# Copying PSUM banks into a transposed weight table with the tokens innermost, in a decoder layer's expert stage

## The chip, the cores and the metric

The kernel runs on one core of one Trainium2 chip. The metric is the device time of one execution in microseconds (us). TensorE (PE) multiplies and writes its products to PSUM, in banks of 512 fp32 columns; VectorE (DVE), ScalarE (ACT) and GpSimd (POOL) work beside it; SyncE (SP) and GpSimd issue the transfers. Each engine works through its own queue in order, and waits where an input or a buffer isn't ready.

## The reference

One decoder layer on 512 tokens of width 1024. A mixing part (sparse attention and a gated linear recurrence) gives `h`. Then comes the part that matters here, a retrieval over 16384 experts, each a row of `u` and a row of `v`:

```python
experts = jnp.take_along_axis(cand_idx..., pos, axis=-1)      # 8 heads x 16 per token
g = jax.nn.softmax(best, axis=-1)
h = jax.nn.gelu(jnp.einsum('td,thkd->thk', xb, u[experts]))
return jnp.einsum('thk,thkd->td', g * h, v[experts])
```

Every token picks 128 experts, and expert numbers are pairs (i, j) with i and j below 128. The result is added to the scaled `h` and normalised.

## The kernel before, in words

The 512 tokens are four blocks of 128. For blocks 0 and 1 the kernel gathers the chosen rows: `gather` lets GpSimd fetch one row of `u` or `v` per token (512 KB in all) into a tile `g`, VectorE multiplies and sums it (L665 for `u`, tile `gu`; L678 for `v`, tile `gv`). A generator, `peer_gather`, yields after each such row, and `pump(n)` in the other stages takes n of them. 52 of the v rows of block 0 go another way, through TensorE, in `pe_gather`: ScalarE makes a 128x128 diagonal `dg` with the gates of one choice (L694), and TensorE multiplies the gathered tile by it, two products of 512 columns (L696), summed in two banks (`pv` for the first 14 choices, `pw` for the other 38).

Blocks 2 and 3 (256 tokens) go through all 16384 experts densely, in `dense`. First the G stage builds a table G of shape [128 (i), 128 (j), 256 (token)], which holds the gate of expert (i, j) for every token. It takes four tokens at a time, a group; there are 64 groups. For each, VectorE compares `iota` with the token's 128 i and 128 j numbers and makes two tiles of one-hots `og` (L749); the second is multiplied by the gates, token by token, by ScalarE (L753), or for some tokens by VectorE (L755); TensorE multiplies the two for each of the four tokens into a bank `gb` laid out (token, j) (L758); ScalarE copies the bank of the group before into G (L736). Every second group one token of `pe_gather` follows, eight (PEPRE) having been taken before the stage; every third group (GPUMP) one row of block 1's `u` is pumped. `dtr` holds the transposed numbers and gates of the blocks, copied from PSUM by ScalarE (L727) just before.

Then the hidden stage runs over the 128 j: it streams 1 MB of `u` and `v` for each j, splits them into two parts, multiplies (L785), weighs with `G[:, j, :]` (L791) and multiplies again into four banks (L805). It pumps the remaining gathered rows on the way.

The gathered tiles share four buffers (tag `g`) in the G stage. `og` has 4 and 6 buffers, `gb` two, `dg` one; the `u` tiles of the hidden stage take over the buffers of `og`. The framework's planner orders the instructions of each engine and hands out buffers ahead of time, by a timeline of its own; where the text says `keep_in_program_order`, the order is as written.

Of the kernel before, what the change touches and what calls it, by code (L numbers as in the profile page):

```python
# [9 lines left out]
F32 = mybir.dt.float32  # L10
# [16 lines left out]
HGB = 5  # L27
GB = 4
UB = 4
VB = 3  # L30
HLB = 6
KB2 = 11
# [8 lines left out]
PEPRE = 8  # L41
PEG = 60

GACTS = (3, 4)

GPUMP = 3

# [4 lines left out]
def tile_decoder_layer(ctx, tc, a, out):  # L52
    nc = tc.nc

    cst = ctx.enter_context(tc.tile_pool(name="cst", bufs=1))
    gat = ctx.enter_context(tc.tile_pool(name="gat", bufs=5))
# [577 lines left out]
    def gather(table, b, k, nm):  # L634
        n = nth[0] % (GB + len(lent))
        nth[0] += 1
        if n < GB:
            t = gat.tile([128, 1024], F32, name=f"g{nm}{b}_{k}", tag="g", bufs=GB)
        else:
            t = cst.tile([128, 1024], F32, name=f"g{nm}{b}_{k}", tag=lent[n - GB])  # L640
        nc.gpsimd.indirect_dma_start(out=t, out_offset=None, in_=table,  # L641
                                     in_offset=bass.IndirectOffsetOnAxis(ap=idx[b][k // 64][:, k % 64:k % 64 + 1], axis=0))
        return t
# [42 lines left out]
    def pe_gather(n, p):  # L686

        while 0 not in weighted:
            pump(1)
        ks = [pe_left.pop(0) for _ in range(n)]  # L690
        for k in ks:
            g = gather(a["v"], 0, k, "v")
            dg = gat.tile([128, 128], F32, name=f"dg{k}", tag="dg", bufs=1)
            nc.scalar.mul(dg, ident, gate[:, 0, k:k + 1])  # L694
            for i in range(2):
                nc.tensor.matmul(p[i], dg, g[:, i * 512:(i + 1) * 512], start=(k == ks[0]), stop=(k == ks[-1]))  # L696
            if k != ks[-1]:
                yield
        for i in range(2):
            y = hs[0][:, i * 512:(i + 1) * 512]  # L700
            nc.vector.tensor_tensor(y, y, p[i], op=ALU.add)
        yield
# [4 lines left out]
    def pump(n):  # L707
        while n > 0 and todo:
            try:
                if not next(todo[0]):  # L710
                    return
                n -= 1
            except StopIteration:
                todo.pop(0)

    def dense(den, dps):
# [5 lines left out]
        for i, b in enumerate(DENSE):  # L722
            p = dps.tile([128, 512], F32, name=f"dtp{b}", tag="gb", bufs=2)
            for n, src in enumerate((keep[b][0], keep[b][1], gate[:, b, :])):
                nc.tensor.transpose(p[:, n * 128:(n + 1) * 128], src, ident)
            t = den.tile([128, 4, 128], F32, name=f"dtr{b}", tag="v", bufs=VB)
            nc.scalar.copy(t[:, 0:3, :].rearrange("p a b -> p (a b)"), p[:, :384])  # L727
            tr[b] = [t[:, n, :] for n in range(3)]
        pw = pe_gather(PEK2, [dps.tile([128, 512], F32, name=f"pw{n}", tag=f"acc0_{n}") for n in range(2)])
        for _ in range(PEPRE):  # L730
            next(pw)
        pdone = PEPRE
        G = den.tile([128, 128, T], F32, name="G")

        def evacuate(t0, p):
            nc.scalar.copy(G[:, :, t0:t0 + 4].rearrange("p j t -> p t j"), p)  # L736

        def pump_some(t0):
            if t0 // 4 % GPUMP == 0:
# [2 lines left out]
        for t0 in range(0, T, 4):  # L742
            p = dps.tile([128, 4, 128], F32, name=f"gb{t0}", tag="gb", bufs=2)
            x = tr[DENSE[t0 // 128]]
            c = t0 % 128
            og = [den.tile([128, 4, 128], F32, name=f"og{t0}_{n}", tag=tag, bufs=bufs)
                  for n, (tag, bufs) in enumerate((("u", UB), ("hl", HLB)))]
            for n in range(2):
                nc.vector.tensor_tensor(og[n], iota[:, None, :].to_broadcast([128, 4, 128]),  # L749
                                        x[n][:, c:c + 4, None].to_broadcast([128, 4, 128]), op=ALU.is_equal)  # L750
            gact = GACTS[t0 // 4 % len(GACTS)]
            for tt in range(gact):
                nc.scalar.mul(og[1][:, tt, :], og[1][:, tt, :], x[2][:, c + tt:c + tt + 1])  # L753
            if gact < 4:
                nc.vector.tensor_tensor(og[1][:, gact:, :], og[1][:, gact:, :],  # L755
                                        x[2][:, c + gact:c + 4, None].to_broadcast([128, 4 - gact, 128]), op=ALU.mult)
            for tt in range(4):
                nc.tensor.matmul(p[:, tt, :], og[0][:, tt, :], og[1][:, tt, :], start=True, stop=True)  # L758
            if t0:
                evacuate(t0 - 4, last)  # L760
            last = p
            pump_some(t0)
            while pdone < PEK2 and pdone < PEPRE + (t0 // 4 + 1) * (PEK2 - PEPRE) // PEG:
                next(pw)
                pdone += 1
        evacuate(T - 4, last)
        while 0 not in spent:
            pump(1)
# [10 lines left out]
        def into_hidden(j, n, hp):  # L779
            u = den.tile([128, 512], F32, name=f"u{j}_{n}", tag="u", bufs=UB)  # L780
            nc.sync.dma_start(u.rearrange("p (k i) -> p k i", k=4), a["ut"][j, :, n * 4:n * 4 + 4, :])
            uh, ul = split(f"u{j}_{n}", u)
            for q, (ut, ht) in enumerate(((uh, hTl), (uh, hTh), (ul, hTh))):
                for k in range(4):
                    nc.tensor.matmul(hp, ut[:, k * 128:(k + 1) * 128], ht[n][:, k, :],  # L785
                                     start=(n + q + k == 0), stop=(n == 1 and q == 2 and k == 3))
# [11 lines left out]
        def out_of_hidden(j, n, wh, wl):  # L798
            v = den.tile([128, 512], F32, name=f"v{j}_{n}", tag="v", bufs=VB)
            nc.sync.dma_start(v, a["v"][j * 128:(j + 1) * 128, n * 512:(n + 1) * 512])  # L800
            vh, vl = split(f"v{j}_{n}", v)
            for i in range(nb):
                sl = slice(i * 128, (i + 1) * 128)
                for q, (wt, vt) in enumerate(((wl, vh), (wh, vh), (wh, vl))):
                    nc.tensor.matmul(acc[i][n], wt[:, sl], vt, start=(j == 0 and q == 0), stop=(j == 127 and q == 2))  # L805

        def residual():
            ia = gat.tile([128, 128], F32, name="ia", tag="dg", bufs=1)
            nc.scalar.mul(ia, ident, ALPHA)
            for i in range(nb):  # L810
                for n in range(2):
                    for c in range(4):
                        for t in (hTl, hTh):
                            nc.tensor.matmul(acc[i][n][:, c * 128:(c + 1) * 128],
                                             t[n].bitcast(F32)[:, c, i * 128:(i + 1) * 128], ia,
                                             start=False, stop=False)
# [4 lines left out]
        for j in range(129):  # L821
            if j < 128:
                hp = dps.tile([128, 512], F32, name=f"hp{j}", tag="hp", bufs=2)[:, :T]
                into_hidden(j, 0, hp)
            want = total * min(j + 1, DLAST) // DLAST
            pump(want - due)
            due = want
            if j:
                out_of_hidden(j - 1, 0, *ws)
            if j == 2:  # L830
                residual()
            if j == DLAST:
                gb = ln2_consts(1)
                finish(1, gb)
            if j < 128:
                into_hidden(j, 1, hp)
                ws_new = weigh(j, hp)
            if j:
                out_of_hidden(j - 1, 1, *ws)
            ws = ws_new  # L840
# [5 lines left out]
    def stage(blocks, xT):  # L846
# [39 lines left out]
        if blocks != [0]:  # L886
            lent.clear()
            for part, tags in (("h", ("hx0", "hx1")), ("l", ("hs2", "hs3"))):
                hT_parts[part] = [cst.tile([128, 4, 256], F32R, name=f"hT{part}{i}", tag=tag) for i, tag in enumerate(tags)]
            for k in range(0, 8, 2):  # L890
                x = hT[:, k:k + 2, 128:384]
                th, tl = [hT_parts[part][k // 4][:, k % 4:k % 4 + 2, :] for part in "hl"]
                nc.scalar.copy(th, x)
                nc.vector.tensor_tensor(tl, x, th.bitcast(F32), op=ALU.subtract)
            for _ in pe_gather(PEK1, [bank(f"pv{i}", "hg") for i in range(2)]):
                pass
# [58 lines left out]
```

## Time and profile before

| what | value |
|---|---|
| time, median of 3 runs | 1610.61 us (1610.09 to 1612.2) |
| the profiled execution | 1619.35 us, span 1617.6 us |
| mean granted TensorE clock | 0.942 |
| busy share of the span: PE, DVE, ACT, POOL | 89%, 86%, 44%, 42% |
| DMA | 467.90 MB, 289 GB/s in the mean |

The span is the time from the first instruction to the last in one execution under the profiler; the time of that execution is a little longer than its span. The runs without a profiler are those of the median. PEld is TensorE's loading of weights, which overlaps its products. Shares over the whole span hide that the stages have different limits, so the rows further down are of single stretches.

### The profile page before, as it was taken

The page shows a single profiled execution, that of the slowest core. Times are in us where ns is not written, and L with a number is a line of the kernel's source. Part 1 is how long each engine was busy: PE and PEld are TensorE (multiplying, and loading weights), DVE is VectorE, ACT ScalarE, POOL GpSimd, SP SyncE. Part 2 cuts the span into 40 slices and gives each one's busy share as a digit, 9 for nine tenths or more (in the row PEclk, how much of TensorE's full clock was granted, in tenths as well). Part 3 has the DMA queues.
Part 4 walks back from the last instruction along what each step waited for, and adds up shares of the span by engine and source line. Part 5 has one row for each costly group of instructions (what it writes and reads, how often), then busy time and mean ns, then how long its engine had stood idle before and what let it go on. Part 6 is the DMA issues. An engine that isn't in the chain of part 4 may idle for free. (4 is left out here: it accounts for less than half of the span.)

```text
span 1617.6 us, 24516 instructions
## 1 busy us (share of the span) xinstructions
PE 1446.4 (89%) x7858; PEld 1090.0 (67%) x7858; DVE 1385.0 (86%) x3263; ACT 707.1 (44%) x1501; POOL 674.6 (42%) x531
## 2 busy tenths in 40 slices
PE   8997879755777799679989999999999999999996
PEld 4756534533443466236668888888888889989985
DVE  4219997888889889998887999899998999999998
ACT  3312121122332012249994555555555555555553
POOL 0000057757766440254443444444453346545440
PEclk9998989865789899999999999999999999999998
DMA  8454579989879871457678999999999999999995
GB/s 289 171 161 150 171 265 409 341 304 346 301 270 342 309 296 53 143 164 229 225 226 289 350 345 354 320 351 351 354 352 332 342 343 361 358 348 351 353 360 192
DMA packets 166162, 467.90 MB, mean 289 GB/s; under 512 B 18576, under 2 KB 18704, under 8 KB 165904
## 3 DMA queue, kind: packets, MB, share of 16 engines
q0 software_dynamic: 73728, 268.47, 47.4%
q1 hardware_dynamic: 92304, 197.86, 33.9%
q8 instruction: 62, 1.02, 0.2%
q14 instruction: 68, 0.56, 0.1%
HBM read 464.16 MB, written 2.10 MB: 288 GB/s over the span
## 5 line engine op out<-in xcount | busy, mean ns | idle before, releaser
L641 POOL DMA_INDIRECT gv<-in_v_dram,idx x256 | 340.8, 1331 | 400.4 <-DVE hs L678 237.5
L641 POOL DMA_INDIRECT gu<-in_u_dram,idx x256 | 323.0, 1262 | 433.3 <-DVE gu L665 193.0
L665 DVE SCALAR_TENSOR_TENSOR gu<-gu,hs 128x1024 f32<-128x1024 f32 x256 | 310.9, 1236 | 30.5 <-DMA gu<-in_u_dram,idx 30.0
L678 DVE SCALAR_TENSOR_TENSOR hs<-gv,gate,hs 128x1024 f32<-128x1024 f32 x204 | 261.5, 1282 | 12.1 <-DMA gv<-in_v_dram,idx 9.3
L774 ACT CAST v_0h<-v 128x512 fp32r<-128x512 f32 x128 | 79.7, 623 | 95.3 <-PE acc L805 57.9
L525 PE MATMUL pq<-hT,wpq 128*128 128x128 f32 (+1 forms) x512 | 118.4, 389 | 0.0
L774 ACT CAST v_1h<-v 128x512 fp32r<-128x512 f32 x128 | 79.5, 621 | 88.6 <-DMA v<-in_v_dram 40.2
L776 DVE TENSOR_TENSOR u_0l<-u,u_0h 128x512 fp32r<-128x512 f32 x128 | 88.5, 691 | 29.6 <-ACT u_0h L774 26.7
L774 ACT CAST u_0h<-u 128x512 fp32r<-128x512 f32 x128 | 79.3, 620 | 68.0 <-PE hp L785 32.1
L805 PE MATMUL acc<-v_0h,wl 128*128 128x512 f32 x256 | 102.0, 399 | 2.8 <-DVE wl L795 2.8
L776 DVE TENSOR_TENSOR v_1l<-v,v_1h 128x512 fp32r<-128x512 f32 x128 | 88.1, 688 | 17.2 <-ACT v_1h L774 13.9
L525 PEld LDWEIGHTS pq<-hT,wpq 128*128 128x128 f32 x512 | 79.9, 198 | 31.7 <-issue 1.1
L805 PE MATMUL acc<-v_0h,wh 128*128 128x512 f32 x256 | 101.2, 395 | 0.0
L774 ACT CAST u_1h<-u 128x512 fp32r<-128x512 f32 x128 | 79.4, 621 | 49.5 <-PE acc L805 42.1
L805 PE MATMUL acc<-v_1h,wl 128*128 128x512 f32 x256 | 100.3, 392 | 0.0
L805 PE MATMUL acc<-v_1h,wh 128*128 128x512 f32 x256 | 100.1, 391 | 0.0
L805 PE MATMUL acc<-v_0l,wh 128*128 128x512 f32 x256 | 99.7, 391 | 0.0
L776 DVE TENSOR_TENSOR u_1l<-u,u_1h 128x512 fp32r<-128x512 f32 x128 | 88.0, 687 | 5.8 <-ACT wh L793 2.3
L776 DVE TENSOR_TENSOR v_0l<-v,v_0h 128x512 fp32r<-128x512 f32 x128 | 88.2, 689 | 2.5 <-ACT v_0h L774 1.5
L785 PE MATMUL hp<-hTh,u_1l 128*128 128x256 f32 x512 | 84.8, 288 | 4.9 <-DVE u_1l L776 2.9
L785 PE MATMUL hp<-hTl,u_0h 128*128 128x256 f32 x512 | 83.8, 286 | 6.0 <-ACT u_0h L774 5.7
L785 PEld LDWEIGHTS hp<-hTl,u_0h 128*128 128x128 f32 x512 | 76.4, 189 | 18.6 <-ACT u_0h L774 8.8
(275 smaller groups left out, 3199.3 us busy)
## 6 DMA issues: line engine op xcount, KB each, us to landing
v<-in_v_dram SPq DMA_DIRECT2D x256, 256.0 KB
u<-in_ut_dram SPq DMA_DIRECT2D x256, 256.0 KB
wpq<-in_w_pq_dram SPq DMA_DIRECT2D x32, 512.0 KB
wo<-in_w_o_dram SPq DMA_DIRECT2D x16, 512.0 KB
hfw<-in_w_hf_dram SPq DMA_DIRECT2D x8, 512.0 KB
hqw<-in_w_hq_dram SPq DMA_DIRECT2D x8, 512.0 KB
hiw<-in_w_hi_dram SPq DMA_DIRECT2D x8, 512.0 KB
qaw<-in_w_qa_dram SPq DMA_DIRECT2D x8, 512.0 KB
```

The costliest lines, as they stand in the source:

```text
L525: nc.tensor.matmul(qp[:, :nt], w[:, k, :], hT[:, k, :nt], start=(k == 0), stop=(k == 7))
L641: nc.gpsimd.indirect_dma_start(out=t, out_offset=None, in_=table, in_offset=bass.IndirectOffsetOnAxis(ap=idx[b][k // 64][:, k % 64:k % 64 ...
L665: nc.vector.scalar_tensor_tensor(g, g, 1.0, hs[b], op0=ALU.mult, op1=ALU.mult, accum_out=hd[:, k:k + 1]))
L678: nc.vector.scalar_tensor_tensor(hs[b], g, gate[:, b, k:k + 1], hs[b], op0=ALU.mult, op1=ALU.add))
L774: nc.scalar.copy(h, x)
L776: nc.vector.tensor_tensor(l, x, h.bitcast(F32), op=ALU.subtract)
L785: nc.tensor.matmul(hp, ut[:, k * 128:(k + 1) * 128], ht[n][:, k, :], start=(n + q + k == 0), stop=(n == 1 and q == 2 and k == 3))
L805: nc.tensor.matmul(acc[i][n], wt[:, sl], vt, start=(j == 0 and q == 0), stop=(j == 127 and q == 2))
```

## The change

Three edits, all in the G stage or shared with it.

The copy of a bank into G goes through its elements in another order. Before, it went token by token, reading the bank in its own order and writing with a step of 256 elements (1024 bytes) between neighbours. Now it goes through j, and for each j through the four tokens: it writes four neighbouring elements of G, then steps by 256 elements, and reads the bank with a step of 128 elements (512 bytes). What ends up in G is the same.

ScalarE multiplies the one-hots of all four tokens of each group by the gates. Before, it took three in every even group and four in every odd one, and VectorE took the remaining one.

The diagonals `dg` get two buffers in place of one. The scaled identity of the residual (`ia`) shares them.

```diff
+DGB = 2
...
-GACTS = (3, 4)
+GACTS = (4,)
...
-            dg = gat.tile([128, 128], F32, name=f"dg{k}", tag="dg", bufs=1)
+            dg = gat.tile([128, 128], F32, name=f"dg{k}", tag="dg", bufs=DGB)
...
         def evacuate(t0, p):
-            nc.scalar.copy(G[:, :, t0:t0 + 4].rearrange("p j t -> p t j"), p)
+            nc.scalar.copy(G[:, :, t0:t0 + 4], p.rearrange("p t j -> p j t"))
...
-            ia = gat.tile([128, 128], F32, name="ia", tag="dg", bufs=1)
+            ia = gat.tile([128, 128], F32, name="ia", tag="dg", bufs=DGB)
```

## Rows read from the trace of the kernel before

**Rows 1.** Windows: length; busy us (instructions) of PE, PEld, DVE, ACT, POOL; clock; DMA.
```profile
640.00:713.00 73.00, 55.32 (x145) 23.92 (x143) 72.21 (x452) 20.01 (x39) 24.36 (x18) 0.95 0.41 123
713.00:850.00 137.00, 124.14 (x644) 84.77 (x644) 116.43 (x216) 131.34 (x324) 62.96 (x56) 0.99 0.71 228
870.00:1600.00 730.00, 720.11 (x4548) 648.37 (x4547) 673.88 (x1096) 389.94 (x757) 323.69 (x225) 1.00 0.96 343
```

**Rows 2.** Waits of PE, 870 to 1600: total us, times, longest.
```profile
PE hp L785 <- ACT u_0h L774: 4.0, 11, 0.9
```

**Rows 3.** Groups of ACT, 713 to 850: busy us, mean ns, idle before, releaser.
```profile
L753 ACT ACTIVATE og<-og,dtr 128x128 f32<-128x128 f32 x224 | 73.0, 412 | 0.0
L736 ACT COPY G<-gb 128x512 f32<-128x512 f32 x64 | 64.9, 1072 | 1.7 <-PE gb L758 1.7
L694 ACT ACTIVATE dg<-ident,gate 128x128 f32<-128x128 f32 x32 | 13.2, 412 | 5.5 <-PE pw L696 5.5
L727 ACT COPY dtr<-dtp 128x384 f32<-128x384 f32 x2 | 0.8, 469 | 0.0
```

**Rows 4.** Timeline of ACT, 795 to 800: start, us, what, times, idle before.
```profile
795.68 1.94 ACT L736 COPY G<-gb 128x512 f32<-128x512 f32 x2
797.41 1.27 ACT L753 ACTIVATE og<-og,dtr 128x128 f32<-128x128 f32 x4
798.58 0.40 ACT L694 ACTIVATE dg<-ident,gate 128x128 f32<-128x128 f32 x1
798.87 0.99 ACT L753 ACTIVATE og<-og,dtr 128x128 f32<-128x128 f32 x3
799.74 1.02 ACT L736 COPY G<-gb 128x512 f32<-128x512 f32 x1
```

**Rows 5.** Groups of ACT over the whole span, copies out of PSUM.
```profile
L455 ACT COPY PT<-pt 128x512 f32<-128x512 f32 x20 | 10.7, 591 | 6.0 <-PE pt L453 6.0
...
L527 ACT COPY pqs<-pq 128x128 f32<-128x128 f32 x16 | 4.3, 267 | 19.6 <-PE pq L525 19.6
```

**Rows 6.** Timeline of ACT at the start of the G stage.
```profile
712.93 0.84 ACT L727 COPY dtr<-dtp 128x384 f32<-128x384 f32 x2
715.16 0.40 ACT L694 ACTIVATE dg<-ident,gate 128x128 f32<-128x128 f32 x1 [1.39 <-PE pw L696]
...
722.26 1.06 ACT L736 COPY G<-gb 128x512 f32<-128x512 f32 x1 [1.08 <-PE gb L758]
```

**Rows 7.** Groups of DVE, 713 to 850.
```profile
L665 DVE SCALAR_TENSOR_TENSOR gu<-gu,hs 128x1024 f32<-128x1024 f32 x22 | 26.9, 1223 | 16.6 <-DMA gu<-in_u_dram,idx 16.6
L755 DVE TENSOR_TENSOR og<-og,dtr 128x128 f32<-128x128 f32 x32 | 9.1, 285 | 0.2
```

**Rows 8.** Timeline of PE before the stage, one token of 14 such.
```profile
672.97 1.98 PE L696 MATMUL pv<-gv,dg 128*128 128x512 f32 x4 [0.55 <-ACT dg L694]
```

**Rows 9.** Timeline of PE, 733 to 742.
```profile
734.14 1.88 PE L696 MATMUL pw<-gv,dg 128*128 128x512 f32 x4
735.86 1.95 PE L758 MATMUL gb<-og,og 128*128 128x128 f32 x16
737.64 1.88 PE L696 MATMUL pw<-gv,dg 128*128 128x512 f32 x4
```

**Rows 10.** Waits of DVE, 713 to 850: total us, times, longest.
```profile
DVE gu L665 <- DMA gu<-in_u_dram,idx: 16.6, 15, 3.1
```

**Rows 11.** Timeline of DVE, 800 to 832, the products with gathered u.
```profile
807.00 1.23 DVE L665 SCALAR_TENSOR_TENSOR gu<-gu,hs 128x1024 f32<-128x1024 f32 x1 [0.86 <-DMA gu<-in_u_dram,idx]
...
813.19 1.22 DVE L665 SCALAR_TENSOR_TENSOR gu<-gu,hs 128x1024 f32<-128x1024 f32 x1 [0.78 <-DMA gu<-in_u_dram,idx]
...
819.04 1.23 DVE L665 SCALAR_TENSOR_TENSOR gu<-gu,hs 128x1024 f32<-128x1024 f32 x1 [0.77 <-DMA gu<-in_u_dram,idx]
```

**Rows 12.** Timeline of POOL, two issues of gathers of u.
```profile
776.50 1.85 POOL L641 DMA_INDIRECT gu<-in_u_dram,idx  x1 [2.37 <-PE pw L696]
...
808.51 1.35 POOL L641 DMA_INDIRECT gu<-in_u_dram,idx  x1 [2.16 <-DVE og L755]
```

## Prediction

> **What bounds the kernel now.** I read the sums by stretch first [rows 1]. The edits touch the G stage, 713 to 850 us, where ScalarE is busy 131.3 of 137.0 us, TensorE 124.1 and VectorE 116.4. So ScalarE sets the pace there, with TensorE close behind. The stretch before it (640 to 713) belongs to VectorE, 72.2 of 73.0 us. The one behind it (870 to 1600) belongs to TensorE, 720.1 of 730.0 us, and its longest wait there on any one line is 4.0 us in all [rows 2]. That stretch runs a fixed amount of work and starts when G is full, so what the G stage gains or loses is passed on to the end about one for one.
>
> Next, the groups of ScalarE inside the stage [rows 3]: 224 weights of one-hots, 64 copies into G, 32 diagonals. Their idle times are 0, 1.7 and 5.5 us. Mean durations overlap their neighbours, so I take start to start from the timeline [rows 4]. Two copies start at 795.68 and the next weight at 797.41, so a copy takes 0.865 us of the engine. Four weights fill 797.41 to 798.58, 0.293 each; the diagonal takes 0.29; the pattern repeats at 799.74. A pair of groups (eight tokens) therefore costs 4.06 us. The sum, 64 x 0.865 + 224 x 0.293 + 32 x 0.29 = 55.4 + 65.6 + 9.3 = 130.3, with 0.8 for the two dtr copies, is the 131.3 of [rows 1].
>
> **The copies.** How much of 0.865 is due to the order of the elements? The same instruction with both sides contiguous stands elsewhere in the kernel [rows 5]: 512 columns out of PSUM take 591 ns, 128 columns 267, so 0.844 ns per column and a fixed 159. The copy into G moves the same 512 columns in 1072 ns [rows 3], 1.78 ns per column: about twice as much. Its read is contiguous; its write steps 1024 bytes from element to element, so the scattered write is what doubles it. After the edit the write has runs of four elements (16 bytes), and the read steps 512 bytes through a PSUM bank on every element. No row here shows ScalarE reading PSUM with such a step.
>
> So I bound it. Below: the contiguous price. Two dtr copies of mean 469 ns end 0.84 us after the first started [rows 3, 6], so the second started 0.37 us after the first and contiguous copies overlap by 0.10; the edited copy would take 0.591 - 0.10 = 0.49 us, and 64 of them give back 64 x 0.375 = 24.0 us. Above: the stepped read costs what the stepped write cost, 0.865, and nothing is given back. Both penalties at once (0.48 us more on top of 0.865, 31 us in all) is the far end; I leave it out of the forecast, since the write would have to keep its price although three of four elements follow their neighbour. I take 0.49: the only measured penalty goes with the write.
>
> [...]
>
> **The weights.** Every second group hands one weight from VectorE to ScalarE: 32 more at 0.293, so +9.4 us on ScalarE, and VectorE loses 32 x 285 ns = 9.1 us [rows 7]. VectorE isn't the bound by its busy time, so that gives nothing back by itself. ScalarE's new sum is 31.4 + 75.0 + 9.3 = 115.7, against 130.3: 14.6 us less, 3.61 us per pair.
>
> **The diagonals.** With one buffer, TensorE waits 0.55 us for each diagonal when it does nothing but such tokens: the product at 672.97 shows it, as do 13 more between 640 and 713 us [rows 8]. A second buffer removes this. Before 713 us that is worth nothing, because VectorE's routing covers it; without that cover it would be 14 x 0.55 = 7.7 us. At the stage's start it should help: ScalarE sits 1.39 us for a diagonal's buffer and 1.08 us for the first bank, because TensorE is still at the last two tokens of the eight taken in advance [rows 6]. I count 1 us of these 2.5: how much of them is TensorE's lateness and how much VectorE's first one-hots, the rows don't part. In the stage proper, ScalarE can place a diagonal earlier in its queue; as long as ScalarE is the bound that gives nothing. The residual's scaled identity shares this buffer and isn't waited for.
>
> **What is late next.** TensorE: a token (1.72) and eight products (1.78) run back to back from 734.14 to 737.64, 3.50 us for a pair [rows 9]. 30 pairs with a token and two without make 30 x 3.50 + 2 x 1.78 = 108.6 us. That is below 115.7, so it caps little. VectorE: 116.4 - 9.1 = 107.3 us busy, but it also waits 16.6 us for gathered rows of u, in 15 of 22 cases [rows 7, 10]. This is the cap that matters. In the second half of the stage each gather of u is issued right behind the product that used the one before: VectorE starts one at 807.00 and ends 1.15 us later; GpSimd issues the next at 808.51; it has landed at 813.19 [rows 11, 12]. The loop is 0.35 + 4.68 + 1.15 = 6.2 us, and 5.85 the next time (813.19 to 819.04), 6.02 on average, and the work of three groups that lies between two of them has 1.5 x 4.06 = 6.09 us now. Behind the waiting product stand VectorE's next one-hots, and behind these ScalarE's weights and TensorE's products. So where the gathers of u go round in one buffer, a faster ScalarE finds VectorE at 6.02 us per three groups, hardly faster than today. In the first half a gather of u also takes over the buffer of a v row, as the one at 776.50 does when a token's products are over [rows 12], and this loop doesn't bind.
>
> **The sum.** First half, 16 pairs: 16 x 0.45 = 7.2 us gained. Second half, 11 gathers: 11 x (6.09 - 6.02) = 0.8. Start: 1. Friction where ScalarE and TensorE come within 0.1 us of each other: I take 1 off. Together 8 us: the profiled span 1617.6 would become 1609.6. The profiled execution took 1619.35, 0.5% above the median of 1610.6; the G stage is a fixed piece of work, so I take the same 8 us off the median: 1602.5.
>
> **The rivals.**
> 1. *No gather loop binds.* The order of the gathers and who inherits which buffer are settled ahead by the framework's planner, and the edits change its input. If u gathers alternate buffers throughout, all 32 pairs gain 0.45, with the start 15 us: 1595 to 1599. For it: the first half before behaves so. Against it: the second half.
> 2. *The read takes the write's place* (the other side). The PSUM read with its 512-byte step costs two steps per element, the copy stays at 0.865, and 9.4 us of weights come on top: 1610.6 + 9.4 - 1 = 1619. It decides from a copy of 0.865 - 9.4 / 64 = 0.72 us start to start; above that the edit loses. [...] Against it: no row shows a slow PSUM read.
> 3. *The gather loop binds everywhere.* 22 x 6.02 = 132 us against the stage's 137: with the start and the tail the time moves by 0 to 3 us, 1607.5 to 1611. For it: VectorE already waits in 15 of 22 cases.
>
> **How the numbers follow.** The likeliest, 1598 to 1606 round 1602.5, has 0.36; rival 1 has 0.24; rival 3 has 0.17; rival 2 has 0.20; 0.03 is for a far worse copy. 0.2%, about what can be told from no change, is 3.2 us. Faster: 0.36 + 0.24 + a third of rival 3 = 0.66. Same: the rest of rival 3 and a copy near 0.72, 0.14. Slower: 0.20. The range: 1595 leaves out the lower end of rival 1 (0.05), and 1617 most of rival 2 and the far case (0.15). The likeliest's own range is 1598 to 1606.
>
> **What would show it.** The copy into G: about 590 ns mean, and 0.49 start to start, if the step on the PSUM side is free; 1070 if not. 256 weights on ScalarE, none on VectorE. ScalarE's busy sum in the stage near 116, its stage some 127 to 130 us long. VectorE's wait for rows of u grows from 16.6 us if the loop binds; if not, TensorE's idle in the stage shrinks instead. The 0.55 us before each diagonal's product is gone before 713, and the VectorE bound there unmoved. The prediction is wrong if the copy stays above 0.72, or if the stretch behind 870 us changes its own length.

## The result, and the profile after

The changed kernel takes 1638.69 us (median of 4 runs, 1632.59 to 1642.45) beside 1610.35 us for the kernel before on the same chip (4 runs): a ratio of 1.0171, 95% interval 1.0146 to 1.0196. It is 28 us slower where 8 us of gain was predicted, and lies above the range. The profiled execution took 1638.91 us, span 1637.2 us. All lines below the diagonals' buffer count stand one lower in the file than before: the copy into G is L737, the products L697 and L759, the one-hots L750.

I count the stage from the first copy into G to the last: 722.3 to 848.0 before, 125.7 us. In the changed kernel, by windows (columns as in [rows 1]):

```profile
640.00:713.00 73.00, 56.24 (x131) 24.20 (x129) 65.69 (x402) 19.25 (x42) 28.30 (x25) 0.91 0.56 178
713.00:863.00 150.00, 119.81 (x637) 86.48 (x638) 109.75 (x189) 117.52 (x348) 52.40 (x49) 0.94 0.58 181
720.40:861.90 141.50, 113.43 (x617) 82.31 (x617) 101.86 (x173) 115.48 (x343) 50.68 (x47) 0.96 0.60 187
884.00:1610.00 726.00, 714.26 (x4512) 643.53 (x4511) 666.07 (x1078) 385.23 (x750) 322.79 (x225) 1.00 0.96 344
```

The third row is the stage: 141.5 us, 15.8 more. No engine is busy for more than 115.5 of them. Before, ScalarE had 131.3 of 137.0 [rows 1]; now nobody has the stage. The last row is as before, TensorE busy 98% of it. Of the span's 19.6 us the stage holds 15.8; the first to the last weighing by G in the hidden stage takes 747.1 us beside 743.5, and 0.2 net lie at the start, the gap and the tail. The other 8.7 of the 28 us stand in no trace: the profiled execution of the kernel before took 1619.35 us, 9 above its median.

The groups of ScalarE, 713 to 863 us, against [rows 3]:

```profile
L754 ACT ACTIVATE og<-og,dtr 128x128 f32<-128x128 f32 x256 | 81.6, 395 | 4.0 <-DVE og L750 4.0
L737 ACT COPY G<-gb 128x512 f32<-128x512 f32 x64 | 36.0, 575 | 5.4 <-PE gb L759 4.8
L695 ACT ACTIVATE dg<-ident,gate 128x128 f32<-128x128 f32 x25 | 10.0, 398 | 22.9 <-PE pw L697 22.8
```

The copy fell from 1072 to 575 ns, and all 256 weights are ScalarE's. Its timeline, against [rows 4]:

```profile
739.78 0.56 ACT L737 COPY G<-gb 128x512 f32<-128x512 f32 x1
740.25 2.44 ACT L754 ACTIVATE og<-og,dtr 128x128 f32<-128x128 f32 x8
```

A copy is 0.47 us start to start (739.78 to 740.25), where 0.49 was forecast. So the copies do what they should; ScalarE waits instead, 22.9 us for the buffers of diagonals, which TensorE still reads. Who is late? The waits of all engines, 713 to 863 us (us in total, times, longest), against [rows 10]:

```profile
DVE og L750 <- PE gb L759: 40.1, 19, 4.8
POOL gu L642 <- DVE gu L666: 31.9, 7, 9.6
POOL gu L642 <- PE pw L697: 27.3, 9, 7.5
PE pw L697 <- DMA gv<-in_v_dram,idx: 26.6, 14, 4.4
ACT dg L695 <- PE pw L697: 22.8, 10, 4.8
```

VectorE's 16.6 us for rows of u are gone. It waits 40.1 us for TensorE to release the one-hots, TensorE waits 26.6 us for gathered rows of v, and GpSimd, which issues these, waits for VectorE and TensorE. That is a ring. One turn of it, first on TensorE:

```profile
820.16 1.99 PE L697 MATMUL pw<-gv,dg 128*128 128x512 f32 x4 [2.84 <-DMA gv<-in_v_dram,idx]
821.98 2.89 PE L759 MATMUL gb<-og,og 128*128 128x128 f32 x24
824.70 1.88 PE L697 MATMUL pw<-gv,dg 128*128 128x512 f32 x4
826.42 1.05 PE L759 MATMUL gb<-og,og 128*128 128x128 f32 x8
827.31 1.88 PE L697 MATMUL pw<-gv,dg 128*128 128x512 f32 x4
829.03 1.95 PE L759 MATMUL gb<-og,og 128*128 128x128 f32 x16
833.84 1.55 PE L697 MATMUL pw<-gv,dg 128*128 128x512 f32 x3 [2.87 <-DMA gv<-in_v_dram,idx]
```

then on VectorE:

```profile
823.07 2.50 DVE L750 TENSOR_TENSOR og<-iota,dtr 128x512 f32<-128x512 f32 x4 [2.96 <-PE gb L759]
825.48 1.22 DVE L666 SCALAR_TENSOR_TENSOR gu<-gu,hs 128x1024 f32<-128x1024 f32 x1
```

and on GpSimd:

```profile
826.98 1.15 POOL L642 DMA_INDIRECT gu<-in_u_dram,idx  x1 [3.63 <-DVE gu L666]
828.43 0.94 POOL L642 DMA_INDIRECT gv<-in_v_dram,idx  x1 [0.30 <-issue]
```

Follow the bracketed waits. TensorE's token at 820.16 and the first group behind it let VectorE write one-hots at 823.07 (2.91 us). Four of them stand in VectorE's queue ahead of the product with u at 825.48 (2.41). GpSimd wants that product's buffer for its next row of u and issues at 826.98 (1.50). The row of v that TensorE needs next has its own buffer, but stands behind in the same queue: 828.43 (1.45). It lands for TensorE at 833.84 (5.41). The sum is 13.68 us for six groups, 4.56 us a pair, where before a pair took 4.06. Also new are the 24, 8 and 16 products between tokens (3, 1 and 2 groups); before, it was 16 from the third gap on [rows 9]. TensorE's wait of 2.8 to 2.9 us ends at 806.50, at 820.16 and at 833.84, so this turn stands there twice in a row; earlier in the stage the order varies.

### The profile page after: what moved, and what is told of

It reads as the page before. It is cut to its first block, busy times and chain, and to the rows that moved or that the text cites. A ratio compares the mean times of both kernels' runs of the same rounds, so it can differ in the third digit from the quotient of the medians.

```text
span 1637.2 us, 24560 instructions
## 1 busy us (share of the span) xinstructions
PE 1455.2 (89%) x7858; PEld 1099.5 (67%) x7858; DVE 1378.4 (84%) x3231; ACT 695.0 (42%) x1533; POOL 671.0 (41%) x531
## 5 line engine op out<-in xcount | busy, mean ns | idle before, releaser
L642 POOL DMA_INDIRECT gu<-in_u_dram,idx x256 | 327.2, 1278 | 450.5 <-DVE gu L666 221.2
L642 POOL DMA_INDIRECT gv<-in_v_dram,idx x256 | 333.0, 1301 | 403.4 <-DVE hs L679 239.0
L750 DVE TENSOR_TENSOR og<-iota,dtr 128x512 f32<-128x512 f32 x128 | 81.1, 686 | 46.3 <-PE gb L759 40.1
L697 PE MATMUL pw<-gv,dg 128*128 128x512 f32 x152 | 82.3, 675 | 40.1 <-DMA gv<-in_v_dram,idx 33.1
L777 DVE TENSOR_TENSOR v_1l<-v,v_1h 128x512 fp32r<-128x512 f32 x128 | 88.0, 687 | 20.7 <-ACT v_1h L775 19.2
```

The source lines that it names most:

```text
L777: nc.vector.tensor_tensor(l, x, h.bitcast(F32), op=ALU.subtract)
```

## The experiments

**Theory**: the copy and the weights cost what was predicted; the stage is long because rings over the shared gather buffers close, and because the edits moved the order in which TensorE takes its tokens. **Rivals**: one of the edits is dear on its own engine (ScalarE's 115.7 us binds, or the weights cost more there), or TensorE's lower granted clock (0.94 in the second window beside 0.99 in [rows 1]) is the cause and not the result. All kernels compute the whole reference. "Stage" is the first to the last copy into G in the profiled execution; ratios are to the kernel before on the same chip, with 95% intervals. Medians of the kernel before move between 1610 and 1618 us from one batch of runs to the next, and single runs of one kernel by 10 to 23 us, so stages part the theories better than times, though each stage is that of one execution. The change itself was timed in the first batch alone. The first copy lies between 714.6 and 730.4 us (722.3 before), which the stage leaves out.

**One edit at a time.**

```diff
+DGB = 1
+GACTS = (3, 4)
```

(e1, the copy's order alone; e2 is the kernel before with `DGB = 2` alone; e3 is the copy with `GACTS = (4,)` and `DGB = 1`; e4 the copy with `GACTS = (3, 4)` and `DGB = 2`.)

> The copy's element order alone; weights and diagonals as before, and no instruction changes its place in any queue. If the ring of gathers behind the second diagonal buffer is the cause (theory A): ScalarE's 64 copies cost 575 ns in place of 1072 and the time falls by 5 to 13 us, 1598 to 1606. If any faster ScalarE runs into the gathers (theory B): the time stays or rises, 1608 to 1635, with TensorE waiting for rows of v as it does after the change.

> The second diagonal buffer alone; copy and weights as before. Theory A: slower by 15 to 30 us, 1626 to 1640, with TensorE's tokens waiting for rows of v some 20 to 30 us in the G stage. Theory B: within 5 us of before, since ScalarE still sets the pace at 4.06 us per pair.

> Copy and weights as in the change, one diagonal buffer. Theory A: faster than before by 5 to 14 us, 1596 to 1606. Theory B: near the changed kernel, 1625 to 1640. Theory C (the weights moved to ScalarE are what hurts): slower than the copy alone by 10 us or more.

> Copy and second diagonal buffer as in the change, weights shared with VectorE as before. Theory A: near the changed kernel, 1625 to 1642. Theory C: near the copy alone, 1598 to 1606.

| kernel | stage, us | ratio |
|---|---|---|
| before | 125.7 | 1 |
| e1, copy | 119.6 | 0.9976 (0.9944 to 1.0008) |
| e2, second diagonal buffer | 136.8 | 1.0074 (1.0039 to 1.0109) |
| e3, copy and weights | 133.6 | 1.0048 (1.0016 to 1.0080) |
| e4, copy and second buffer | 135.7 | 1.0089 (1.0063 to 1.0115) |
| the change | 141.5 | 1.0171 (1.0146 to 1.0196) |

The copy alone gains 4 us where theory A had 5 to 13, not clear of noise. e2 and e4 lose as theory A has it, but less: e2 11.7 us where 15 to 30 were expected, e4 about half of the change's loss. e3 goes against theory A, which had a gain, and meets theory C: it is 12.7 us slower than the copy alone, so the weights hurt too.

The second buffer, costed at nothing, makes the kernel before slower by itself. e2 and e4 have the same stage within 1.1 us although ScalarE is busy 125.9 us in the one and 105.6 in the other, so ScalarE doesn't set it. The waits of e2, 713 to 863 us, are of the kinds of the changed kernel; the most goes to rows of u that take over the buffer of a row of v and wait for TensorE's token (27.3 us in the changed kernel):

```profile
POOL gu L642 <- PE pw L697: 40.1, 12, 7.5
POOL gv L642 <- PE pw L697: 30.0, 16, 2.7
DVE og L750 <- PE gb L759: 25.1, 13, 5.2
PE pw L697 <- DMA gv<-in_v_dram,idx: 23.3, 13, 4.8
```

What the second buffer does to TensorE's queue can be counted in the timelines. In e2 and e4, 12 tokens stand ahead of the first group and the last 11 groups have no token between them; in the change it is 12 and 13, in the kernel before, e1 and e3 8 and 5. Between these ends e2 and e4 keep a token after every second group, as before, so the 3, 1 and 2 groups are not needed for the loss. The end of e2's tokens:

```profile
841.45 1.88 PE L697 MATMUL pw<-gv,dg 128*128 128x512 f32 x4
843.17 1.95 PE L759 MATMUL gb<-og,og 128*128 128x128 f32 x16
845.59 1.16 PE L759 MATMUL gb<-og,og 128*128 128x128 f32 x8 [0.47 <-ACT G L737]
```

e3 has another ring. Its waits and its window, 718.3 to 851.9 us:

```profile
POOL gu L642 <- DVE gu L666: 55.7, 15, 8.3
DVE gu L666 <- DMA gu<-in_u_dram,idx: 30.5, 18, 3.3
ACT og L754 <- DVE og L750: 18.6, 17, 2.4
```
```profile
718.30:851.90 133.60, 115.66 (x623) 81.09 (x621) 102.98 (x170) 113.57 (x342) 50.60 (x49) 1.00 0.65 210
```

Rows of u go round in one buffer from the stage's start to its end, 133.6 / 22 = 6.07 us a row. From one product with u to the next, over half of the turns take 5.9 to 6.3 us; four take 8.1 to 8.3, because a row of v has taken over u's buffer and the next row of u stands behind it (shown for e12 below). The shorter loop is the one that the prediction read at 6.02 [rows 11, 12] and let bind in the second half.

The clock here is 1.00 in a stage nearly as long as e2's. In the changed kernel it is lower only in pieces:

```profile
715.00:719.00 4.00, 3.88 (x6) 1.85 (x7) 4.00 (x8) 0.10 (x1) 0.00 (x0) 0.50 0.00 0
800.00:860.00 60.00, 46.55 (x280) 35.16 (x279) 48.01 (x84) 50.18 (x149) 22.17 (x20) 1.00 0.58 184
```

The turn shown above lies in the second piece, at 1.00: that ring isn't made by the clock. An estimate from the mean of 0.96 over the stage: the clock can hold at most 0.04 x 141.5 = 5.7 of its us.

**Buffers parted by use.** In the G stage, rows of v get two of the four buffers, rows of u two.

```diff
-            t = gat.tile([128, 1024], F32, name=f"g{nm}{b}_{k}", tag="g", bufs=GB)
+            tag = ("g", "gx")[nm == "u" if in_g[0] else n % 2]
+            t = gat.tile([128, 1024], F32, name=f"g{nm}{b}_{k}", tag=tag, bufs=GB // 2)
```

> The whole change, with the four gather buffers parted in the G stage: two for rows of v, two for rows of u (elsewhere they alternate). Theory A (the loss is the ring: rows of u and v inherit each other's buffers, so GpSimd's queue waits for VectorE and TensorE in turn): the G stage, first copy into G to last, falls from 141 us to 118 to 125 and the time is 10 us or more under the changed kernel's. Theory D (a stage this fast can't be fed with gathered rows, whoever inherits the buffers): the stage stays at 133 us or more, and TensorE's tokens still wait over 15 us for rows of v.

> The kernel before, with the buffers parted in the same way; the control for the run above. Both theories: ScalarE sets the pace at 4.06 us per pair, the stage stays at 124 to 130 us, and the time stays within 4 us of before.

> The copy's element order alone, with the buffers parted. Theory A: the stage falls below the 119.6 us of the copy alone, to 113 to 118, and the time is 3 to 6 us under the copy alone. Theory D: no better than the copy alone, 119 us or more.

On the change (e5) the stage falls only to 133.1 us, ratio 1.0060 (1.0032 to 1.0088). TensorE still waits for v, 20.7 us from 713 to 855, and GpSimd 49.7 us for TensorE to release a buffer: two are too few for v in that order. This is what theory D had. On the kernel before (e6): 129.6 us, 0.9976 (0.9954 to 0.9999). On the copy alone (e7): 122.0 us, 0.9959 (0.9933 to 0.9985); theory A had 113 to 118 for it.

**No rows of u in the stage.** `GPUMP = 64` moves 21 of the 22 rows of u from the G stage into the hidden stage.

> The whole change with all but one of block 1's 22 rows of u moved out of the G stage into the hidden stage, which gets them as extra work. Theory A: with rows of v alone in the four buffers nobody inherits from the other kind, and the G stage falls from 141 us to 113 to 122; the hidden stage grows. Theory D: TensorE still waits for rows of v and the stage stays above 130.

One run: 1624.7 us beside 1615.16. The stage is 124.8 us, above the 113 to 122 expected, and TensorE waits for no row of v in it. That fits rows of u closing the ring, but doesn't show it: the order of TensorE's tokens came out otherwise too (16 ahead of the first group, two after every second group, none between the last 43). The hidden stage takes 752.5 us between its first and last weighing, 5 to 16 more than in the others, with the 21 rows as extra work.

**A fifth gather buffer**, in the room of the hidden stage's split weights, which isn't in use yet: three for v, two for u.

```diff
+        if in_g[0] is not None:
+            in_g[1] += nm == "u"
+            if nm == "u" and in_g[1] % 2:
+                t = in_g[0].tile([128, 1024], F32, name=f"g{nm}{b}_{k}", tag="whl")
+            else:
+                t = gat.tile([128, 1024], F32, name=f"g{nm}{b}_{k}", tag="gx" if nm == "u" else "g", bufs=1 if nm == "u" else 3)
...
-            wh = den.tile([128, T], F32R, name=f"wh{j}", tag="wh", bufs=2)
+            wh, wl = (whl[0][:, 2 * k + j % 2, :].bitcast(F32R) for k in range(2))
```

(e9 is the change with it, e10 the copy alone, e11 the kernel before, e13 copy and weights, e14 copy and second diagonal buffer.)

> The whole change with a fifth gather buffer in the G stage (the room of wh and wl, which only the hidden stage uses): three buffers for rows of v, two for rows of u. Theory A (a ring of too few, shared buffers): no gather waits long for a buffer, TensorE's tokens wait under 6 us for rows of v in the stage, and the stage falls from 141 us to 116 to 124; the time is 15 us or more under the changed kernel's. Theory D (the gathers themselves are too slow for such a stage): over 130 us.

> The copy's element order alone, with the five parted buffers. Theory A: the stage, 119.6 us with the copy alone and 122.0 with four parted buffers, falls to 111 to 117, TensorE's sum being 108.6; the time is 8 to 16 us under before. Theory D: 119 or more.

> The kernel before with the five parted buffers, the control. Both theories: ScalarE's sum of 130 us keeps the stage at 124 to 128 us; the time stays within 5 us of before.

> Copy and weights as in the change, one diagonal buffer, five parted gather buffers. If the 133.6 us of copy and weights together are the loop of rows of u, the stage falls to ScalarE's own sum, 115 to 119 us; the 32 weights then cost 5 to 9 us against the copy alone with the same buffers (109.8). If the weights hurt by something else, 125 or more.

> Copy and second diagonal buffer as in the change, weights shared, five parted buffers. If the planner's order of the tokens costs by itself (tokens taken early, bare groups left for the end), the stage is 115 to 122 us against 109.8 without the second buffer; if the second buffer hurts only through the ring of gathers, 108 to 112.

| kernel | stage with 4, us | stage with 5, us | ratio with 5 |
|---|---|---|---|
| before (e11) | 125.7 | 125.2 | 1.0011 (0.9990 to 1.0033) |
| copy (e10) | 119.6 | 109.8 | 0.9918 (0.9892 to 0.9943) |
| copy and weights (e13) | 133.6 | 118.5 | 0.9985 (0.9962 to 1.0008) |
| copy and second buffer (e14) | 135.7 | 127.7 | 1.0065 (1.0036 to 1.0094) |
| the change (e9) | 141.5 | 123.1 | 1.0029 (1.0009 to 1.0048) |

The fifth buffer gives the kernel before nothing: there ScalarE bound. Behind the faster copy it gives 8 to 18 us of stage. e9, e11 and e13 lie in the stages expected, e10 1.2 us under, e14 above both of its ranges. The windows of e10 and e13:

```profile
717.40:827.20 109.80, 107.94 (x618) 78.40 (x616) 106.84 (x200) 103.63 (x307) 53.81 (x49) 1.00 0.79 253
```
```profile
725.50:844.00 118.50, 111.50 (x618) 79.72 (x616) 102.42 (x172) 112.03 (x339) 54.61 (x49) 0.99 0.73 234
```

In e10 TensorE is busy 107.9 of 109.8 us: the prediction's sum for TensorE, 108.6, is the stage. In e13 no engine waits long for a gathered row, and the stage is 118.5 - 109.8 = 8.7 us longer with the 32 weights; ScalarE's busy time grows by 8.4 us, for 9.4 predicted, and its sum was 115.7. In e13's stage TensorE also waits for the next diagonal in the one buffer:

```profile
PE pw L705 <- ACT dg L703: 6.6, 7, 2.8
```

e9 and e14, the two with the second diagonal buffer, are still too long with next to no wait for rows. Near the end of e9's stage TensorE works groups without any token between them (L768 is its product of one-hots):

```profile
837.32 1.16 PE L768 MATMUL gb<-og,og 128*128 128x128 f32 x8 [0.49 <-ACT G L745]
838.98 1.16 PE L768 MATMUL gb<-og,og 128*128 128x128 f32 x8 [0.50 <-ACT G L745]
```

With the second buffer, TensorE's queue takes a token after every group until 782 us (2.61 us a group, its own pace) and has none left for the last 41 groups. These go at ScalarE's pace, four weights and a copy, 1.66 us (837.32 to 838.98). Two engines that were to overlap take turns instead.

**Fewer rows of u in the stage, four buffers**: e3 with `GPUMP = 4`.

> Copy and weights as in the change, one diagonal buffer, and rows of u pumped after every fourth group in place of every third (16 in the stage, 6 more in the hidden stage). With a loop of 6.07 us per row of u as the cause of the 133.6 us of copy and weights together, 16 x 6.07 = 97 no longer binds and the stage falls to 117 to 122. If the 32 extra weights on ScalarE are the cause, it stays at 130 or more.

One run, 1611.44 us beside 1615.85; the stage is 129.2 us, so the expectation missed: the loop grew as its turns became fewer. VectorE's timeline shows the turn, 770.08 to 778.47, 8.39 us for four groups (16 such would be 134):

```profile
770.08 1.23 DVE L666 SCALAR_TENSOR_TENSOR gu<-gu,hs 128x1024 f32<-128x1024 f32 x1 [2.16 <-DMA gu<-in_u_dram,idx]
...
778.47 1.23 DVE L666 SCALAR_TENSOR_TENSOR gu<-gu,hs 128x1024 f32<-128x1024 f32 x1 [2.31 <-issue]
```

and GpSimd's shows why:

```profile
771.59 1.14 POOL L642 DMA_INDIRECT gv<-in_v_dram,idx  x1 [2.46 <-DVE gu L666]
773.04 0.93 POOL L642 DMA_INDIRECT gu<-in_u_dram,idx  x1 [0.30 <-PE gb L759]
```

Here a row of v inherits u's buffer and waits for VectorE's product, and the next row of u, whose buffer is free, stands behind it.

**TensorE's order held as written.** The products of tokens and of groups in the G stage get `keep_in_program_order`, so a token comes after every second group.

```diff
-                nc.tensor.matmul(p[:, tt, :], og[0][:, tt, :], og[1][:, tt, :], start=True, stop=True)
+                tc.keep_in_program_order(
+                    nc.tensor.matmul(p[:, tt, :], og[0][:, tt, :], og[1][:, tt, :], start=True, stop=True))
```

(and the same for the tokens' products while in the stage. e15 is e9 with it, e16 the change itself with its four buffers, e17 is e14, e18 is e5.)

> The whole change with five parted buffers, and TensorE's queue in the G stage held to the order of the text: one token after every second group. If the order of the tokens is what is left (123.1 us in place of 116), the stage falls to 115 to 119 us, ScalarE's sum; if not, it stays at 121 or more.

> The changed kernel with its four shared buffers, and only TensorE's queue in the G stage held to the order of the text: a token of the v rows after every second group, where the changed kernel had 3, 1 and 2 groups between tokens. Theory A (the order of the tokens closes the loop over TensorE): the waits for rows of v shrink to under 8 us and the stage takes 116 to 126 us, since what is left is ScalarE's 115.7 or part of the loop of u; ratio to before 0.99 to 1.00. Theory B (who inherits which buffer closes it, a row of v queued behind a waiting row of u in GpSimd's queue): the waits stay at some 15 to 27 us, the stage at 131 to 142 us, ratio 1.005 to 1.018. What is nearer to B says that the buffers are the cause and the order only shapes it.

> The copy's order and the second diagonal buffer, five gather buffers, and TensorE's queue in the G stage held to the order of the text. Without the hold this took 127.7 us in the stage and 1.0065 of the time before. If the order of the tokens is all that was left: stage 109 to 114 us (the copy alone with five buffers 109.8), ratio 0.988 to 0.994, and the second diagonal buffer itself costs nothing. If the second diagonal buffer costs by something else too: stage above 117, ratio above 0.997.

> All three edits, four gather buffers parted in the G stage (two for rows of v, two for rows of u), and TensorE's queue held to the order of the text; no more memory than the changed kernel. With the parting alone the stage was 133.1 us and GpSimd's gathers of v waited 37.4 us for TensorE. If the order is what made two buffers of v too few: stage 114 to 121 us, ratio 0.990 to 0.997. If two buffers of v are too few by themselves (a row lands 4.4 to 5.4 us after its issue, a pair of groups takes 3.6 us): stage 126 to 134, ratio 1.000 to 1.006.

| kernel | stage, order free | stage, order held | ratio, order held |
|---|---|---|---|
| the change (e16) | 141.5 | 130.2 | 0.9993 (0.9969 to 1.0017) |
| parted 2 and 2 (e18) | 133.1 | 125.8 | 0.9976 (0.9954 to 0.9999) |
| five buffers (e15) | 123.1 | 113.1 | 0.9903 (0.9873 to 0.9933) |
| copy, second buffer, five (e17) | 127.7 | 109.3 | 0.9934 (0.9910 to 0.9959) |

In e16 only the order is held, and TensorE has no wait for rows of v left in the stage. What is left is the loop of u in one buffer, 130.2 / 22 = 5.92 us a row; its waits, 717.6 to 847.8 us:

```profile
POOL gu L643 <- DVE gu L667: 63.4, 18, 6.6
...
DVE gu L667 <- DMA gu<-in_u_dram,idx: 27.7, 18, 2.8
...
POOL gu L643 <- PE pw L698: 2.4, 1, 2.4
```

So the expectation's theory A holds for the ring over TensorE, but its 116 to 126 us missed: it left out that the loop of u would still bind. The last line shows that the hold also changed who inherits which buffer: rows of u wait 2.4 us for TensorE, where in the change's stage they waited 19.8. So e16 doesn't part the order from the inheritance. With parted buffers neither kind of row can inherit from the other, and there the hold gives 7.3 us (e18), 10.0 (e15) and 18.4 (e17). With two buffers for v (e18) GpSimd still waits 34.6 us for TensorE, and the 125.8 us lie between the two ranges expected. With five buffers, no long wait for a gathered row is left in e15 or e17; e17's 109.3 equals e10's 109.8, so with the order held the second diagonal buffer costs nothing there, where TensorE is the bound. The window of e15:

```profile
715.50:828.60 113.10, 110.97 (x621) 77.53 (x620) 103.45 (x174) 110.76 (x339) 55.10 (x49) 1.00 0.74 240
```

TensorE and ScalarE are both busy 111 of 113.1 us, less than the 115 to 119 expected. TensorE's order in e15 is the same as in e13, which has one diagonal buffer; TensorE's 6.6 us of waits for diagonals are gone, the stage is 5.4 us shorter, and the ratio 0.9903 stands beside 0.9985. (The profiled spans differ by 15.3 us; 10.0 of them lie ahead of the first copy, and why is not shown.) So with all weights on ScalarE, the order held and the buffers parted, the kernel with the second buffer is the faster one. e15 (1602.22 us beside 1618.29) and e10 (1602.78 beside 1615.85) beat both kernels.

## Why the prediction was wrong, step by step

**What bounds, and that the stage passes its time on**: right in the main. In the kernels above, the weighings of the hidden stage span 737 to 747 us whatever the G stage did, except in e8, which moved work there. That spread of 10 us is as large as most of the gains and losses, so single spans don't show them one for one.

**The copies**: right, 0.47 us for 0.49. The second rival, a stepped read as dear as the stepped write, is out: its price was an estimate from the write [rows 3], and no run shows two steps per element for such a read. ScalarE's copy with a read step of 512 bytes and a write in runs of 16 bytes took 575 ns here, where copies with both sides contiguous took 591 [rows 5] and the write step of 1024 bytes had cost 1072 [rows 3].

**The weights**: right in size, 8.4 us of ScalarE's time from e10 to e13 and 8.9 from e17 to e15, for 9.4. The stage pays 8.7 us in the one pair and 3.8 in the other. But they also changed the planner's choice of buffers: from e1 to e3 the loop of u went from part of the stage to all of it, and the stage from 119.6 to 133.6 us.

**The diagonals**: this is the first step that failed. "In the stage proper, ScalarE can place a diagonal earlier in its queue; as long as ScalarE is the bound that gives nothing." It costed the second buffer by ScalarE's queue alone. The buffer count is an input of the planner: with two, TensorE's queue comes out in another order (12 tokens ahead of the first group in place of 8) and rows of v wait behind rows of u. Alone it cost 11.1 us of stage (e2 against before), behind the copy 16.1 (e4 against e1). With the order held the changed kernel is 0.9993 (e16): by the ratio the whole of the loss is gone, by the profiled stages 11.3 of the 15.8 us, and the rest is the loop of u. With five buffers and the order held nothing of the second buffer's cost is left (e17), and with all weights on ScalarE the kernel with it is the faster one (e15 beside e13).

**What is late next**: the loop of u was found, and its 6.02 us was right for over half of the turns (5.9 to 6.3 in e3 and e16); the turns of up to 8.3 us were not in it. The second step that failed is where it was taken to bind. "In the first half a gather of u also takes over the buffer of a v row" was read from the order before, and carried over, though the first rival said that the edits change it. With the copy alone it did carry over: 16 pairs at TensorE's 3.50 and 11 turns of 6.02 make 122 us, and e1's stage is 119.6. With the weights it did not: e3, without the second buffer, is 1.0048. So either failed step alone turns the forecast gain into a loss.

**The range**: the third rival, the loop of u in the whole stage, was priced at 0 to 3 us of gain. It set 22 x 6.02 = 132 us against the window of 137, but from the first copy to the last the stage had been 125.7, so 132 is a loss of 6 to 7. e3 bears this out: 133.6 us, 1.0048. e16, with 130.2 us, has 0.9993, near the price, but as its stage is 4.5 us longer than before, that is luck as far as its profile tells. The range ended at 1617 because every loop considered ran through VectorE alone, and none was much longer than the 6.09 us that ScalarE took before. A ring through GpSimd's queue, TensorE and VectorE together, 13.68 us where ScalarE had taken 12.2, was not among the cases; TensorE's pace, the loop over VectorE and the waits in GpSimd's queue stood in [rows 9, 11, 12], its order did not.

**Open**: in the profiles the change's stage and e16's differ by 11.3 us, their ratios by more, 1.8%; e16's profiled execution is the slowest of its ten, and the rest is not accounted for. Nor is it why e3 and e16, with nearly the same order and 3.4 us between their stages, differ by 0.55% in their ratios. The copy with the second buffer, four buffers and the order held was not run, so for e4 it is argued, not shown, that the order is the whole cause. Nor was it settled which of the planner's inputs moves a token.

## What to carry to other kernels

Before an engine's sum is taken as the new bound, write down each ring of buffers with every queue that it passes through, and ask which waiting transfer stands ahead of another that is needed sooner: the longest ring is the floor of the stage (in e3 the loop of u, 22 rows at 6.07 us in the mean, was the 133.6 us). A buffer count, or a work split between engines, is also an input of a planner that orders queues and hands out buffers; what the trace shows of an inheritance or an order holds only as long as this input does. When an edit should cost nothing and costs 1%, look first at whether the order of the queue stayed, then hold it, and part the shared buffers by who uses them. An edit that lost may then gain: here the kernel with the second diagonal buffer did (e15 beside e13).

## What the runs showed of the hardware

ScalarE copied 512 columns of a PSUM bank in 575 ns with a read step of 512 bytes and a write in runs of 16 bytes; copies with both sides contiguous took 591 [rows 5], and a step of 1024 bytes on the write side, with a contiguous read, had cost 1072 [rows 3].

TensorE's granted clock in the changed kernel was 0.94 in the mean from 713 to 863 us. It was 0.50 from 715 to 719, right behind a wait of 4.4 us, and 1.00 from 800 to 860, where TensorE waited 2.8 to 2.9 us three times and was busy 46.6 of 60 us. In e3's stage, with TensorE busy 115.7 of 133.6 us and no wait above 1.4 us, it was 1.00, as in e10's, where it was busy 98%.
